# One 256-column value product per key group in a neighbourhood-attention block

## The chip, the core and the metric

The kernel runs on one core of a Trainium2 chip. Its time is the device time of one execution in microseconds (us), median of the runs. The work is spread over TensorE (PE in the profile: matrix products; PEld: loading their stationary operand), VectorE (DVE), ScalarE (ACT), GpSimd (POOL) and SyncE (SP, which here only issues DMAs). Each engine takes its instructions in order and waits on semaphores for the others.

## The reference

One encoder layer over 1024 tokens (a grid of 16 rows and 64 columns) of 1024 channels, in float32:

```python
h = h + 0.5 * swiglu(rms_norm(h, ffn1_norm[i]), ffn1_w_gate[i], ffn1_w_up[i], ffn1_w_down[i])
u = rms_norm(h, mix_norm[i])
q, k, v, s_in, gates = jnp.split(u @ w_in[i], splits, axis=-1)
y_attn = neighbourhood_attention(q, k, v, na_rpb[i]) @ w_attn_out[i]
y_ssm = s5_branch(s_in, ...) @ w_ssm_out[i]
h = h + (sigmoid(gate_a) * y_attn + sigmoid(gate_s) * y_ssm) @ w_out[i]
h = h + 0.5 * swiglu(rms_norm(h, ffn2_norm[i]), ...)
h = h + (p[i] @ ple_w_proj[i]) * jax.nn.sigmoid(rms_norm(h, ple_norm[i]) @ ple_w_gate[i])
return rms_norm(h, final_norm)
```

The attention has 8 heads of 64 channels. Each token sees 8 x 16 neighbours, clamped inside the grid, with a learned bias per head; then softmax over these 128 scores and a weighted sum of the values.

## The kernel before

Activations lie channel-major: 128 channels on the partitions, tokens along the columns. Nearly all products are made in three parts for precision (`mm3`, L182): an operand is split into a rounded part and its remainder (`split`, L152: a cast on ACT, a subtraction on DVE), and hi x hi, hi x lo and lo x hi are summed in PSUM. The order of PE's instructions is the order of the program text (`manual_schedule`, L1796); ACT, DVE and the DMA queues are ordered by a planner that simulates the engines. Only the first stretch and the very end (`end`, L1678) have ACT and DVE in written order as well.

The stages are: feed-forward block 1 (to about 690 us), the mixer (input projections, gates, attention, state-space branch, to about 1170 us), the two branch outputs with gates and the output projection, feed-forward block 2, then the per-layer input and the last norm.

In the mixer the main line of PE is a row of projections (`proj`, L1037: 24 products of 512 columns each) for q, k and the 16 gate tiles. Between these, the generator `mixer_side` (L1286) places the attention and the state-space work: after each so many products `tick` lets it go one step. An attention **unit** is one head, one half of the rows (`rb`) and one of four column blocks (`cb`); there are 64 units, 16 for each pair of heads. In step j the generator puts out:

- the scores of unit j (`attn_scores`, L1198): two products of 288 or 384 columns with the query as the stationary operand; the smallest of the negated scores on DVE (L1211), exponent, sum and scaling on ACT and DVE (L1214 to L1216);
- the turn of unit j-3 (`attn_turn`, L1219): three transposes of 128 columns into one PSUM bank, then a cast on ACT into `pth` (L1226) and the remainder on DVE into `ptl` (L1227);
- the values of unit j-5 (`attn_values`, L1230): for each of three key groups a product of 128 columns with the value's two parts side by side as the stationary operand (128 wide, L1235) and `pth`, and one of 128 columns with the high part alone (64 wide, L1237) and `ptl`. The four column blocks of a head half fill one PSUM bank `O`; after the fourth, ACT copies its lower half out (L1241), DVE adds the upper one in token order (L1242), and ACT issues the store to `o_d` (L1245);
- two steps of the state-space scan on POOL; from unit 49 on also `ssm_out` (L1097), whose products (`yo`) follow the unit's.

`qk_proj` (L1134) makes the operands of two heads: for each head one query tile `qs` of 1024 columns, keys `kh` and `kl`; for each half of the tokens a PSUM bank is copied out by ACT and DVE. Weights, `qs`, `kh`, `kl` and a few others share a ring `w` of 12 tiles of 4 KB per partition; a large ring `x` of 56 tiles of 2 KB holds the normed activations and most short-lived tiles; a ring `tmp` holds four.

`load_br` (L1400) later loads `o_d` for the branch products and splits it. At the end of the program, `rstd` (L204) computes a reciprocal root on ACT and refines it with three DVE steps; `scaled` (L1654) multiplies by a gain on ACT.

Of the kernel before, what the change touches and what calls it, by code (L numbers as in the profile page):

```python
# [8 lines left out]
F32 = mybir.dt.float32  # L9
# [29 lines left out]
def encoder_block(ctx, tc, I, out):  # L39
# [73 lines left out]
    a2_d = dtile("a2_d", [NF // 2, 7, P, HT])  # L113
    h2_d = dtile("h2_d", [P, NK * SEQ])
    v_d = dtile("v_d", [SEQ, 512])
    o_d = dtile("o_d", [512, SEQ])
    g_d = dtile("g_d", [16, P, SEQ])
    y_d = dtile("y_d", [NPD, P, NCH])
    y2_d = dtile("y2_d", [512, SEQ])
# [81 lines left out]

        return tc.issue_after(mark["ins"]) if "ins" in mark else nullcontext()

    def rstd(m, r, q):  # L204
        A.activation(r, m, AF.Abs_reciprocal_sqrt, bias=eps)
        V.tensor_tensor(q, r, r, ALU.mult)
        V.scalar_tensor_tensor(q, m, eps, q, ALU.add, ALU.mult)
        V.scalar_tensor_tensor(r, q, -3.0, r, ALU.add, ALU.mult)

    class Norm:  # L210
# [33 lines left out]
        def stat(self, r=None, summed=False):  # L244
            if summed:
                m = self.acc
            else:
                m = bank("ms")[:, 0:self.n]
                sums = [self.acc] + self.more
                for i, sq in enumerate(sums):  # L250
                    T.matmul(m, lhsT=ones, rhs=sq, start=i == 0, stop=i == len(sums) - 1)
            q = tmq("rq", [P, self.n])
            r = thid("rs", [P, self.n], F32) if r is None else r
            rstd(m, r, q)
            self.r = r

        def apply(self, gi, res, every):
# [774 lines left out]
    win = I["win"]  # L1032
    ap_cm = tc.tile_pool(name="ap", bufs=1, reuse_waits="tile")
    ap_ = ap_cm.__enter__()
    cur.update(st=(ap_, "st", 3), w=(ap_, "w", 12), tmp=(ap_, "tmp", 4))

    def proj(w, t, name):  # L1037
        o = bank(name)
# [95 lines left out]
    def qk_proj(hp, wq, wk):  # L1134
        qs, kh, kl = [], [], []
        for t in range(2):
            o = proj(wq, t, "q")
            for i in range(2):
                if t == 0:
                    qs.append(tw("qs"))  # L1140
                src = o[i * 64:(i + 1) * 64].rearrange("p (r b c) -> p r b c", r=8, b=4)
                hs, ls = slice(i * 64, (i + 1) * 64), slice((1 - i) * 64, (2 - i) * 64)

                def view(sl):
                    return qs[i][sl, hsl(t)].rearrange("p (b r c) -> p r b c", b=4, r=8)
                A.copy(view(hs), src)
                V.tensor_tensor(view(ls), src, view(hs).bitcast(F32), ALU.subtract)
        for t in range(2):
            o = proj(wk, t, "k")
            for i in range(2):  # L1150
                if t == 0:
                    kh.append(tw("kh"))
                    kl.append(tw("kl"))
                hs, ls = slice(i * 64, (i + 1) * 64), slice((1 - i) * 64, (2 - i) * 64)
                A.activation(kh[i][hs, hsl(t)], o[hs], AF.Copy, scale=0.125)
                A.activation(kh[i][ls, hsl(t)], o[hs], AF.Copy, scale=0.125)
                for s_ in (hs, ls):
                    V.scalar_tensor_tensor(kl[i][s_, hsl(t)], o[hs], 0.125, kh[i][hs, hsl(t)].bitcast(F32),
                                           ALU.mult, ALU.subtract)
        for i in range(2):  # L1160
            qkv[2 * hp + i] = (qs[i], kh[i], kl[i])

    def load_v(hd, cb):
        n = 4 * KNC[cb]
# [33 lines left out]
    def attn_scores(hd, rb, cb):  # L1198
        q, kh, kl = qkv[hd]
        n = KNC[cb]  # L1200
        nk = 12 * n
        qv = q[:, rb * HT + cb * P:rb * HT + (cb + 1) * P]

        def kv(kt):
            return kt.rearrange("p (r c) -> p r c", c=GRID)[:, 4 * rb:4 * rb + 12, KC0[cb]:KC0[cb] + n]
# [13 lines left out]
    def attn_turn(cb, sm):  # L1219
        kp = 4 * KNC[cb]  # L1220
        tp = bank("pt")
        for g in range(3):
            T.transpose(tp[0:kp, ksl(g)], sm[:, g * kp:(g + 1) * kp], ident)
# [6 lines left out]
    def attn_values(hd, rb, cb, O, ph, pl):  # L1230
        kp = 4 * KNC[cb]
        hl = vld[hd, cb]
        for g in range(3):

            T.matmul(O[:, ksl(cb)], lhsT=hl[0:kp, rb + g].rearrange("p h d -> p (h d)"), rhs=ph[0:kp, ksl(g)], start=(g == 0), stop=False,  # L1235
                     skip_group_check=True)
            T.matmul(O[0:64, ksl(cb)], lhsT=hl[0:kp, rb + g, 0], rhs=pl[0:kp, ksl(g)], start=False, stop=(g == 2),  # L1237
                     skip_group_check=True)
        if cb == 3:
            ot, ol = tmp("ot"), tmp("ol")  # L1240
            A.copy(ol[0:64], O[64:128])  # L1241
            V.tensor_tensor(ot[0:64].rearrange("p (r b c) -> p b r c", r=8, b=4),  # L1242
                            O[0:64].rearrange("p (b r c) -> p b r c", b=4, r=8),
                            ol[0:64].rearrange("p (b r c) -> p b r c", b=4, r=8), ALU.add)
# [41 lines left out]
    def mixer_side():  # L1286
# [113 lines left out]
    def load_br(t, b):  # L1400

        res = []
        if b == 0:
            for k in range(0, 4, 2):
                st = tst("br")
                nc.sync.dma_start(st.rearrange("p (k c) -> p k c", k=2),
                                  o_d[k * P:(k + 2) * P, hsl(t)].rearrange("(k p) c -> p k c", p=P))
                for i in range(2):
                    hi, lo = tx("bh"), tx("bl")
                    split(hi, lo, st[:, hsl(i)])  # L1410
                    res.append((hi, lo))
            return res
        for k in range(4):
# [264 lines left out]
    def end():  # L1678
# [131 lines left out]
```

## Time and profile before

| | us |
|---|---|
| median of 3 runs | 2099.88 (2099.48 to 2100.86) |
| profiled execution, its own time | 2096.29 |
| its span (first to last instruction) | 2094.5 |
| PE busy | 2074.5 |
| DVE busy | 1416.1 |
| ACT busy | 999.6 |
| POOL busy | 399.4 |

The granted TensorE clock was 0.998. All sums below are made against the profiled execution; its own time is 3.6 us under the median. PE's products are pipelined: the time from one product's start to the next one's start is what it costs, not its own duration. A timeline row reads: start, duration, engine, line, operation, out<-in, rows*columns of the stationary operand, partitions x columns of the moving one, count. A windows row gives, for a stretch, the sum of its length and each engine's busy time and instructions.

### The profile page before, as it was taken

The numbers are of one execution on the slowest core, as the hardware profiler recorded it, in microseconds if no ns is written. First come the engines' busy times: TensorE is split into PE (matmuls) and PEld (weight loads), VectorE is DVE, ScalarE is ACT, GpSimd is POOL, SyncE is SP. The second block draws the span as 40 slices with busy tenths as digits, with TensorE's granted clock in tenths as the row PEclk, the third lists the DMA queues.
The fourth block names the chain that finished last, engine by engine and source line by source line (L and its number), as shares of the span: only waits on it lengthen the run. The fifth ranks groups of instructions, "written<-read, shape, count | busy, mean of one in ns | idle before, by whom it ended". The sixth has DMA issues, their size and how long they took to land.

```text
span 2094.5 us, 28063 instructions
## 1 busy us (share of the span) xinstructions
PE 2074.5 (99%) x9662; PEld 1705.4 (81%) x9662; DVE 1416.1 (68%) x2420; ACT 999.6 (48%) x1832; POOL 399.4 (19%) x636
## 2 busy tenths in 40 slices
PE   8999999999999999999999999999999999999998
PEld 3788888888888888888898888788888888888886
DVE  7897776667967334677753668995665665786855
ACT  6434333334445333667774635643333334445543
POOL 0037556441000006888200001000000000000000
PEclk9999999999999999999999999999999999999999
DMA  3435444475533551233477745243324238433302
GB/s 134 143 118 154 125 135 120 144 270 169 188 114 111 159 189 64 70 97 98 123 208 260 247 145 117 77 150 121 100 86 135 82 121 297 155 106 94 118 21 81
DMA packets 197744, 285.19 MB, mean 136 GB/s; under 512 B 41569, under 2 KB 81121, under 8 KB 197601
## 3 DMA queue, kind: packets, MB, share of 16 engines
q1 hardware_dynamic: 180304, 258.20, 38.8%
q10 hardware_dynamic: 14992, 21.00, 3.0%
q0 software_dynamic: 2304, 4.20, 1.2%
q8 instruction: 76, 1.25, 0.2%
q14 instruction: 68, 0.55, 0.1%
HBM read 201.01 MB, written 82.31 MB: 135 GB/s over the span
## 4 chain that ended last, share of the span: by engine, by line
PE 94%; DVE 2%; ACT 1%; DMA 1%; SPq 0%; issue 0%; DVEq 0%; ACTq 0%
PE dx L184 4%; PE dx L185 4%; PE dx L186 4%; PE gx L184 3%; PE ux L184 3%; PE ux L186 3%; PE gx L186 3%; PE gx L185 3%; PE ux L185 3%; PE gt L184 3%; PE gt L185 3%; PE gt L186 3%; PE dy L186 2%; PE dy L184 2%; PE dy L185 2%; PE gy L184 2%
## 5 line engine op out<-in xcount | busy, mean ns | idle before, releaser
L153 ACT CAST wh<-hbuf 128x512 fp32r<-128x512 f32 x280 | 173.0, 622 | 392.3 <-PE gx L185 80.9
L154 DVE TENSOR_TENSOR wl<-hbuf,wh 128x512 fp32r<-128x512 f32 x280 | 209.2, 750 | 122.7 <-ACT wh L153 120.5
L153 ACT CAST wh<-wblk 128x512 fp32r<-128x512 f32 x190 | 118.0, 622 | 192.6 <-PE dx L185 83.2
L154 DVE TENSOR_TENSOR wl<-wblk,wh 128x512 fp32r<-128x512 f32 x190 | 130.6, 690 | 49.3 <-ACT wh L153 41.8
L184 PE MATMUL dx<-ah,wh 128*128 128x512 f32 x416 | 163.3, 393 | 0.3 <-DVE hbuf L688 0.3
L186 PE MATMUL dx<-ah,wl 128*128 128x512 f32 x416 | 161.9, 389 | 0.0
L185 PE MATMUL dx<-al,wh 128*128 128x512 f32 x416 | 161.8, 389 | 0.0
L1092 POOL TENSOR_TENSOR sc<-X,rho 128x128 f32<-128x128 f32 x128 | 77.9, 609 | 327.2 <-ACT X L1075 317.3
L154 DVE TENSOR_TENSOR al<-araw,ah 128x512 fp32r<-128x512 f32 x154 | 106.3, 694 | 50.1 <-PE dx L185 21.1
L184 PE MATMUL gx<-xh,wh 128*128 128x512 f32 x320 | 124.9, 390 | 1.2 <-DVE c L575 1.2
L184 PE MATMUL ux<-xh,wh 128*128 128x512 f32 x320 | 125.0, 390 | 0.0
L186 PE MATMUL ux<-xh,wl 128*128 128x512 f32 x320 | 124.5, 389 | 0.0
L185 PE MATMUL gx<-xl,wh 128*128 128x512 f32 x320 | 124.5, 389 | 0.0
L186 PE MATMUL gx<-xh,wl 128*128 128x512 f32 x320 | 124.5, 389 | 0.0
L185 PE MATMUL ux<-xl,wh 128*128 128x512 f32 x320 | 124.5, 389 | 0.0
L153 ACT CAST ah<-araw 128x512 fp32r<-128x512 f32 x154 | 94.9, 619 | 43.2 <-PE dx L185 12.6
L184 PE MATMUL gt<-xh,wh 128*128 128x512 f32 x256 | 102.7, 401 | 0.0
L186 PE MATMUL gt<-xh,wl 128*128 128x512 f32 x256 | 99.8, 390 | 0.0
L185 PE MATMUL gt<-xl,wh 128*128 128x512 f32 x256 | 99.8, 390 | 0.0
L422 DVE TENSOR_TENSOR hbuf<-hbuf 128x512 f32<-128x512 f32 x120 | 91.4, 762 | 2.1
L184 PEld LDWEIGHTS dx<-ah,wh 128*128 128x128 f32 x416 | 78.1, 188 | 17.8 <-issue 0.7
L185 PEld LDWEIGHTS dx<-al,wh 128*128 128x128 f32 x416 | 78.1, 188 | 16.9 <-issue 0.7
(381 smaller groups left out, 5590.2 us busy)
## 6 DMA issues: line engine op xcount, KB each, us to landing
araw<-a_d SPq DMA_DIRECT2D x154, 256.0 KB
a_d<-c SPq DMA_DIRECT2D x148, 256.0 KB
wblk<-in_wd SPq DMA_DIRECT2D x88, 256.0 KB
hbuf<-in_wg SPq DMA_DIRECT2D x40, 512.0 KB
hbuf<-in_wu SPq DMA_DIRECT2D x40, 512.0 KB
wst<-in_win SPq DMA_DIRECT2D x26, 512.0 KB
hbuf<-in_xT SPq DMA_DIRECT2D x32, 256.0 KB
h_d<-hbuf ACTq DMA_DIRECT2D x32, 256.0 KB
```

What stands on the lines that cost most here:

```text
L153: A.copy(hi, src)
L154: return eng.tensor_tensor(lo, src, hi.bitcast(F32), ALU.subtract)
L184: T.matmul(o, lhsT=wh, rhs=xh, start=first, stop=False, skip_group_check=more)
L185: T.matmul(o, lhsT=wh, rhs=xl, start=False, stop=False, skip_group_check=more)
L186: T.matmul(o, lhsT=wl, rhs=xh, start=False, stop=last, skip_group_check=more)
L422: V.tensor_tensor(b11, (b12, b22, None, None, b21)[i - 2], b11, ALU.subtract)
L1092: G.tensor_tensor(sc, both, rho4, ALU.mult)
```

## The change

- The turn writes one tile `ptb` of 3 x 2 x 128 columns, high and low part of each key group side by side, in a ring of its own of two tiles. `attn_values` then makes one product of 256 columns for each key group, with the 128-wide stationary operand (the low x low quarter is computed too, and not used). A bank `O` holds two column blocks now instead of four, each with its two parts.
- After each second block ACT copies both halves of the high part into a tile `ot` (one buffer) in token order, and DVE adds the low part to the upper half. `o_d` has two planes: all 128 rows of `ot` are stored, and `load_br` loads both planes and adds them on DVE.
- In `mixer_side` the values of unit j-5 come ahead of the turn of unit j-3.
- Queries are kept by token half, in tiles of the ring `x`; the ring `w` has 10 tiles.
- At the end, two gain multiplications on ACT come behind the reciprocal root (`mid`) instead of ahead of it.

```diff
-    o_d = dtile("o_d", [512, SEQ])
+    o_d = dtile("o_d", [2, 512, SEQ])
...
-    def rstd(m, r, q):
+    def rstd(m, r, q, mid=None):
         A.activation(r, m, AF.Abs_reciprocal_sqrt, bias=eps)
+        if mid is not None:
+            mid()
         V.tensor_tensor(q, r, r, ALU.mult)
...
-    cur.update(st=(ap_, "st", 3), w=(ap_, "w", 12), tmp=(ap_, "tmp", 4))
+    cur.update(st=(ap_, "st", 3), w=(ap_, "w", 10), tmp=(ap_, "tmp", 4))
...
             for i in range(2):
-                if t == 0:
-                    qs.append(tw("qs"))
+                q = thid("qs")
+                qs.append(q)
...
-        qv = q[:, rb * HT + cb * P:rb * HT + (cb + 1) * P]
+        qv = q[rb][:, ksl(cb)]
...
-        ph = thid("pth", [P, 384])
-        pl = thid("ptl", [P, 384])
-        A.copy(ph[0:kp], tp[0:kp, 0:384])
-        V.tensor_tensor(pl[0:kp], tp[0:kp, 0:384], ph[0:kp].bitcast(F32), ALU.subtract)
-        return ph, pl
+        pb = ap_.tile([P, 3, 2, P], F32R, tag="ptb", bufs=2, name="ptb")
+        src = tp[0:kp, 0:384].rearrange("p (g q) -> p g q", g=3)
+        A.copy(pb[0:kp, :, 0], src)
+        V.tensor_tensor(pb[0:kp, :, 1], src, pb[0:kp, :, 0].bitcast(F32), ALU.subtract)
+        return pb
...
+        o = O["o"][:, (cb % 2) * 256:(cb % 2) * 256 + 256]
         for g in range(3):
-            T.matmul(O[:, ksl(cb)], lhsT=hl[0:kp, rb + g].rearrange("p h d -> p (h d)"), rhs=ph[0:kp, ksl(g)], start=(g == 0), stop=False,
+            T.matmul(o, lhsT=hl[0:kp, rb + g].rearrange("p h d -> p (h d)"), rhs=pb[0:kp, g].rearrange("p h q -> p (h q)"), start=(g == 0), stop=(g == 2),
                      skip_group_check=True)
-            T.matmul(O[0:64, ksl(cb)], lhsT=hl[0:kp, rb + g, 0], rhs=pl[0:kp, ksl(g)], start=False, stop=(g == 2),
-                     skip_group_check=True)
+        if cb % 2 == 0:
+            return
+        if cb == 1:
+            O["t"] = ap_.tile([P, HT], F32, tag="ot", bufs=1, name="ot")
+        ov = O["t"].rearrange("p (r b c) -> p b r c", r=8, b=4)[:, cb - 1:cb + 1]
+        src = O["o"].rearrange("p (b h r c) -> p h b r c", b=2, h=2, r=8)
+        A.copy(ov[64:128], src[64:128, 0])
+        A.copy(ov[0:64], src[0:64, 0])
+        V.tensor_tensor(ov[0:64], src[0:64, 1], ov[0:64], ALU.add)
         if cb == 3:
-            ot, ol = tmp("ot"), tmp("ol")
-            A.copy(ol[0:64], O[64:128])
-            V.tensor_tensor(ot[0:64].rearrange("p (r b c) -> p b r c", r=8, b=4),
-                            O[0:64].rearrange("p (b r c) -> p b r c", b=4, r=8),
-                            ol[0:64].rearrange("p (b r c) -> p b r c", b=4, r=8), ALU.add)
-            nc.scalar.dma_start(o_d[hd * 64:(hd + 1) * 64, hsl(rb)], ot[0:64])
+            nc.scalar.dma_start(o_d[:, hd * 64:(hd + 1) * 64, hsl(rb)], O["t"])
...
+            if 0 <= j - 5 < n:
+                hd, rb, cb = units[j - 5]
+                if cb % 2 == 0:
+                    O.setdefault((hd, rb), {})["o"] = bank("O")
+                attn_values(hd, rb, cb, O[hd, rb], pts.pop(j - 5))
+                if rb == 1 and hd + 1 < NH:
+                    load_v(hd + 1, cb)
             if 0 <= j - 3 < n:
                 pts[j - 3] = attn_turn(units[j - 3][2], sms.pop(j - 3))
-            if 0 <= j - 5 < n:
-                hd, rb, cb = units[j - 5]
-                if cb == 0:
-                    O[hd, rb] = bank("O")
-                attn_values(hd, rb, cb, O[hd, rb], *pts.pop(j - 5))
-                if rb == 1 and hd + 1 < NH:
-                    load_v(hd + 1, cb)
...
-                st = tst("br")
-                nc.sync.dma_start(st.rearrange("p (k c) -> p k c", k=2),
-                                  o_d[k * P:(k + 2) * P, hsl(t)].rearrange("(k p) c -> p k c", p=P))
+                st = [tst("br") for _ in range(2)]
+                for w in range(2):
+                    nc.sync.dma_start(st[w].rearrange("p (k c) -> p k c", k=2),
+                                      o_d[w, k * P:(k + 2) * P, hsl(t)].rearrange("(k p) c -> p k c", p=P))
+                V.tensor_tensor(st[0], st[0], st[1], ALU.add)
...
         A.activation(dummy, eps, AF.Abs_reciprocal_sqrt)
-        scaled(6, six[3])
         added(a, b, s, hm)
         fin[2].square(7, V)
-        scaled(7, hm)
         finish(1, (4, 6))
-        fin[2].stat()
+        fin[2].stat(mid=lambda: (scaled(6, six[3]), scaled(7, hm)))
```

On PE, a unit beside a gate tile stood so before (s: scores, pt: transposes, O: values, gt: the gate tile's products):

```order
L186 MATMUL gt<-xh,wl 128x512
L1207 MATMUL s<-kh,qs 128x384
L1208 MATMUL s<-kl,qs 128x384
L1223 MATMUL pt<-ident,sm 96x128 x3
L1235 MATMUL O<-pth,vhl 128x128
L1237 MATMUL O<-ptl,vhl 64x128
L1235 MATMUL O<-pth,vhl 128x128
L1237 MATMUL O<-ptl,vhl 64x128
L1235 MATMUL O<-pth,vhl 128x128
L1237 MATMUL O<-ptl,vhl 64x128
L184 MATMUL gt<-xh,wh 128x512
```

and stands so now:

```order
L186 MATMUL gt<-xh,wl 128x512
L1209 MATMUL s<-kh,qs 128x384
L1210 MATMUL s<-kl,qs 128x384
L1239 MATMUL O<-ptb,vhl 128x256 x3
L1225 MATMUL pt<-ident,sm 96x128 x3
L184 MATMUL gt<-xh,wh 128x512
```

Six products of 128 columns became three of 256, ahead of the transposes; the rest of PE's row is the same in both kernels.

The second place is DVE at the seam between two pairs of heads, from the end of the work behind the scores of unit 15 to those of unit 17, the first that needs the new keys (sm: the row that first reads the scores, kl: the new keys' remainder, of which PE's scores of unit 17 read kl_8033 before and kl_8011 now, wl: a weight's remainder). Before:

```order
L1158 SCALAR_TENSOR_TENSOR kl_8039<-k_7918,kh_8038 64x512 x2
L1215 RECIPROCAL stat_8100<-stat_8100 128x1
L1158 SCALAR_TENSOR_TENSOR kl_8033<-k_8044,kh_8032 64x512 x2
L154 TENSOR_TENSOR wl_8139<-wst_8136,wh_8138 128x1024
L1211 ISA sm_8155,stat_8156<-s_8152,tb_7985 128x288
L1211 ISA stat_8156 128x1
L154 TENSOR_TENSOR wl_8553<-wst_8550,wh_8552 128x1024
L1227 TENSOR_TENSOR ptl_8166<-pt_8161,pth_8165 96x384
```

Now:

```order
L1217 RECIPROCAL stat_8074<-stat_8074 128x1
L1229 TENSOR_TENSOR ptb_8090<-pt_8086,ptb_8090 96x3x128
L154 TENSOR_TENSOR wl_8113<-wst_8110,wh_8112 128x1024
L1213 ISA sm_8129,stat_8130<-s_8126,tb_7968 128x288
L1213 ISA stat_8130 128x1
L1160 SCALAR_TENSOR_TENSOR kl_8011<-k_8022,kh_8010 64x512 x2
L1195 TENSOR_TENSOR tb_8172<-row_8164,colm_6143 128x12x24
L154 TENSOR_TENSOR wl_8503<-wst_8500,wh_8502 128x1024
```

The pair that unit 17 still needs (kl_8033 before, kl_8011 now; the second token half of the pair's first head) stands behind unit 16's score row sm_8129 now, where it stood ahead of it. The pair of the other head's first token half (kl_8039 in the first row before) now stands ahead of unit 15's score row, outside this piece. At unit 33 the rows are the same; at unit 49 two copies of the scan's state stand ahead of the key pair as well.

More of the change, by code (lines that the diff above doesn't have):

```diff
@@ L242, in bring, with stat @@
             self.rest = sq
-        def stat(self, r=None, summed=False):
+        def stat(self, r=None, summed=False, mid=None):
             if summed:
@@ L253, in stat @@
             r = thid("rs", [P, self.n], F32) if r is None else r
-            rstd(m, r, q)
+            rstd(m, r, q, mid)
             self.r = r
@@ L1144, in view @@
                 def view(sl):
-                    return qs[i][sl, hsl(t)].rearrange("p (b r c) -> p r b c", b=4, r=8)
+                    return q[sl].rearrange("p (b r c) -> p r b c", b=4, r=8)
                 A.copy(view(hs), src)
@@ L1160, in qk_proj @@
         for i in range(2):
-            qkv[2 * hp + i] = (qs[i], kh[i], kl[i])
+            qkv[2 * hp + i] = (qs[i::2], kh[i], kl[i])
     def load_v(hd, cb):
@@ L1223, in attn_turn, with attn_values @@
             T.transpose(tp[0:kp, ksl(g)], sm[:, g * kp:(g + 1) * kp], ident)
[L1224 to L1230 removed]
+        pb = ap_.tile([P, 3, 2, P], F32R, tag="ptb", bufs=2, name="ptb")
[3 more added lines that the diff above has]
+        return pb
+    def attn_values(hd, rb, cb, O, pb):
         kp = 4 * KNC[cb]
         hl = vld[hd, cb]
+        o = O["o"][:, (cb % 2) * 256:(cb % 2) * 256 + 256]
         for g in range(3):
[L1235 removed]
+            T.matmul(o, lhsT=hl[0:kp, rb + g].rearrange("p h d -> p (h d)"), rhs=pb[0:kp, g].rearrange("p h q -> p (h q)"), start=(g == 0), stop=(g == 2),
                      skip_group_check=True)
[L1237 to L1245 removed]
+        if cb % 2 == 0:
[7 more added lines that the diff above has]
+        V.tensor_tensor(ov[0:64], src[0:64, 1], ov[0:64], ALU.add)
+        if cb == 3:
+            nc.scalar.dma_start(o_d[:, hd * 64:(hd + 1) * 64, hsl(rb)], O["t"])
     ydr = y_d.rearrange("g (t o) c -> g o t c", o=16)
@@ L1404, in load_br @@
             for k in range(0, 4, 2):
-                st = tst("br")
-                nc.sync.dma_start(st.rearrange("p (k c) -> p k c", k=2),
-                                  o_d[k * P:(k + 2) * P, hsl(t)].rearrange("(k p) c -> p k c", p=P))
+                st = [tst("br") for _ in range(2)]
[3 more added lines that the diff above has]
+                V.tensor_tensor(st[0], st[0], st[1], ALU.add)
                 for i in range(2):
                     hi, lo = tx("bh"), tx("bl")
-                    split(hi, lo, st[:, hsl(i)])
+                    split(hi, lo, st[0][:, hsl(i)])
                     res.append((hi, lo))
```

## The prediction

> **What bounds the kernel now.** I read the page first: its head, the busy times, and the chain of work that ended last (section 4).
>
> ```profile
> span 2094.5 us, 28063 instructions
> PE 2074.5 (99%) x9662; PEld 1705.4 (81%) x9662; DVE 1416.1 (68%) x2420; ACT 999.6 (48%) x1832; POOL 399.4 (19%) x636
> ...
> PE 94%; DVE 2%; ACT 1%; DMA 1%; SPq 0%; issue 0%; DVEq 0%; ACTq 0%
> ```
>
> PE is busy in 99% of the span and is 94% of the chain. An average can hide a stage with another limit, so I looked at the attention's stretch in windows of 20 us (columns: length, then busy time and count of PE, PEld, DVE, ACT, POOL, then clock, DMA share, GB/s).
>
> ```profile
> 880.00:900.00 20.00, 20.00 (x119) 17.39 (x118) 17.62 (x38) 16.38 (x35) 17.26 (x36) 1.00 0.31 91
> 900.00:920.00 20.00, 20.00 (x119) 17.34 (x118) 12.82 (x34) 13.21 (x31) 17.18 (x37) 1.00 0.34 93
> ...
> 1020.00:1040.00 20.00, 19.34 (x131) 17.30 (x131) 12.72 (x36) 12.96 (x31) 0.00 (x0) 1.00 0.58 170
> ...
> 1080.00:1100.00 20.00, 19.60 (x142) 17.74 (x141) 7.32 (x18) 12.86 (x28) 0.00 (x0) 1.00 0.78 233
> ...
> 1120.00:1140.00 20.00, 20.00 (x90) 16.57 (x89) 5.84 (x9) 7.63 (x12) 0.00 (x0) 1.00 0.87 329
> ```
>
> In a quiet stretch (900 to 920) PE is full, DVE stands at 12.8 and ACT at 13.2 of 20. At a seam between two pairs of heads (880 to 900), with new queries and keys to split, DVE is at 17.6 and ACT at 16.4: little room there. PE idles 0.66 us in one window and 0.40 in another, both beside the state-space products. So what PE gives up in this stretch is time won, as long as the other engines keep up.
>
> **The term that counts: the values on PE.** "Busy" says nothing of a small product's cost, since products overlap. I take start to start. This is PE's timeline of one unit behind its scores, and of PEld's stationary loads in it:
>
> ```profile
> 902.01 0.49 PE L1223 MATMUL pt<-ident,sm 128*96 128x128 f32 x3
> 902.25 0.31 PE L1235 MATMUL O<-pth,vhl 128*128 128x128 f32 x1
> 902.39 0.22 PE L1237 MATMUL O<-ptl,vhl 128*64 128x128 f32 x1
> 902.46 0.27 PE L1235 MATMUL O<-pth,vhl 128*128 128x128 f32 x1
> 902.57 0.22 PE L1237 MATMUL O<-ptl,vhl 128*64 128x128 f32 x1
> 902.63 0.27 PE L1235 MATMUL O<-pth,vhl 128*128 128x128 f32 x1
> 902.74 0.23 PE L1237 MATMUL O<-ptl,vhl 128*64 128x128 f32 x1
> 902.80 0.45 PE L184 MATMUL gt<-xh,wh 128*128 128x512 f32 x1
> 903.08 0.40 PE L185 MATMUL gt<-xl,wh 128*128 128x512 f32 x1
> ```
>
> ```profile
> 902.40 0.19 PEld L1235 LDWEIGHTS O<-pth,vhl 128*128 128x128 f32 x1
> 902.51 0.14 PEld L1237 LDWEIGHTS O<-ptl,vhl 128*64 128x64 f32 x1
> 902.57 0.19 PEld L1235 LDWEIGHTS O<-pth,vhl 128*128 128x128 f32 x1
> ```
>
> From the first transpose to the second gate product are 1.07 us. The loads start 0.11 apart behind a 128-wide one and 0.06 behind a 64-wide one, and the products step in the same rhythm (0.11, 0.06): the values are paced by loading their stationary operands, 0.17 per key group.
>
> What the new row costs I put together from two pieces that the trace has. Transposes with a gate tile right behind them, no values, stand at the first units:
>
> ```profile
> 844.65 0.49 PE L1223 MATMUL pt<-ident,sm 128*96 128x128 f32 x3
> 844.89 0.48 PE L184 MATMUL gt<-xh,wh 128*128 128x512 f32 x1
> 845.21 0.39 PE L185 MATMUL gt<-xl,wh 128*128 128x512 f32 x1
> ```
>
> That is 0.56 us from the first transpose to the second gate product. And products of 256 columns with a new 128-wide stationary operand each stand at the end of the program:
>
> ```profile
> 2067.85 0.28 PE L184 MATMUL pg<-xh,whh 128*128 128x256 f32 x1
> 2067.85 0.19 PEld L185 LDWEIGHTS pg<-xl,whh 128*128 128x128 f32 x1
> 2067.97 0.28 PE L185 MATMUL pg<-xl,whh 128*128 128x256 f32 x1
> ```
>
> They start 0.12 apart, each with its own load beside the product before it. Since 0.12 is over the 0.11 of a load, the load is hidden. A unit goes from 1.07 to 3 x 0.12 + 0.56 = 0.92: 0.15 won; with the rounding of the rows 0.15 to 0.16, and I take 0.155. Over 64 units: 64 x 0.155 = **9.9 us**.
>
> The Trainium skill's page "TensorE: Matmul & The Clock Gate" gives, under "Back-to-back issue gap", columns / 2.4 + 2.5 ns, so 109 ns for 256 columns. By that the unit would win 0.18 and the sum would be 11.8 us; the rows above say 0.12, and I stay with them.
>
> **The other terms.** *Copies out of PSUM.* The rows by form, in the attention's stretch (the 128x256 and 128x1024 adds: the program's last stretch):
>
> ```profile
> L1241 ACT COPY ol<-O 64x512 f32<-64x512 f32 x16 | 9.3, 584 | 1.8 <-PE yo L1119 1.5
> ...
> L1121 ACT COPY ys<-yo 128x256 f32<-128x256 f32 x16 | 5.9, 366 | 3.2 <-PE yo L1119 1.8 <-DMA y_d<-ys 1.2
> ```
>
> ```profile
> L1242 DVE TENSOR_TENSOR ot<-O,ol 64x512 f32<-64x512 f32 x16 | 10.9, 680 | 4.3 <-ACT ol L1241 4.2
> ```
>
> ```profile
> L1671 DVE TENSOR_TENSOR hbuf<-hbuf,rs 128x1024 f32<-128x1024 f32 x4 | 4.6, 1220 | 0.0
> ...
> L1651 DVE TENSOR_TENSOR ps<-ps,pp 128x256 f32<-128x256 f32 x4 | 1.7, 414 | 0.0
> ```
>
> ACT had 16 copies of 0.584 (9.3 us) and gets 64 of 256 columns at about 0.366 (23.4): 14 us more over some 265 us, or 1.1 in a window of 20. DVE had 16 adds of 0.680 (10.9) and gets 32 at 0.414 (13.2): 2.4 more. Neither reaches 20 even at a seam (ACT 17.5, DVE 17.8). On the path: nothing, because scores are made three units ahead of their turn, about 11 us; without that cover the 14 us of ACT would be PE's.
>
> *Keys at the seams.* Here the order on DVE moved: the keys that unit 17 needs are behind unit 16's score row now. Times of DVE and PE at this seam:
>
> ```profile
> 890.04 0.29 PE L1207 MATMUL s<-kh,qs 128*128 128x288 f32 x1
> ...
> 893.88 0.29 PE L1207 MATMUL s<-kh,qs 128*128 128x288 f32 x1
> ```
>
> ```profile
> 892.54 0.45 DVE L1211 CUSTOM_DVE_ANT_1 sm<-s,tb 128x288 f32<-128x288 f32 x1
> ...
> 895.18 1.40 DVE L1158 SCALAR_TENSOR_TENSOR kl<-k,kh 64x512 fp32r<-64x512 f32 x2
> ```
>
> DVE came to unit 16's scores 2.50 us after PE had begun them. If it is as late again, the keys behind them (0.45 + 1.40) are ready 4.35 after; PE wants them at 3.84 - 0.155 = 3.69. That is 0.66 lost, three times: 2.0 us. But of the four key remainders (two pairs, 2.8 us) that stood ahead of that row and made it late, none stands between units 15 and 16 now; with DVE only half of that (1.4) earlier there are 0.7 to spare. Between 0 and 2.0 I take 0.3, near the end that the order speaks for.
>
> *Values ahead of the turn.* A part of the weights is used two units after it is made, as before, less the 0.36 that the values now come earlier; that costs nothing against two units of 3.8. The new ring of two tiles costs nothing either: the turn's cast waits for its transposes, and the values that free its tile stand ahead of these on PE.
>
> *One tile `ot`.* Its next first copy must wait for the store of the last contents. A store of 128 KB from ACT's queue is on the chain of waits with
>
> ```profile
> 1031.79 2.98 DMA y_d<-ys
> ```
>
> so 256 KB take 3.0 to 6.0 us (as an estimate: the same, or twice that). With two copies and an add ahead of it (2 x 0.37 + 0.41 = 1.15) that is 4.1 to 7.1, against two units of 3.84 = 7.7. It fits where DVE is not late. I take 0.
>
> *The second plane of `o_d`.* Four DVE adds of 1.22, and 2 MB more each way. In the window 1120 to 1140 PE is full with gates and DVE has 14 us free, so 0.
>
> *The end.* The root on ACT stood behind two gain multiplications:
>
> ```profile
> 2084.47 1.28 DVE L1671 TENSOR_TENSOR hbuf<-hbuf,rs 128x512 f32<-128x512 f32 x2
> 2084.57 0.89 ACT L1655 ACTIVATE hbuf<-hbuf,gains 128x256 f32<-128x256 f32 x2
> 2084.60 0.70 PE L251 MATMUL ms<-sq,ones 128*128 128x256 f32 x2 [0.70 <-DVE sq L232]
> ...
> 2085.85 0.42 DVE L206 TENSOR_TENSOR rq<-rs 128x256 f32<-128x256 f32 x1
> ```
>
> The sum on PE that the root reads ends at 2085.30 anyway, and DVE, which goes on with the root, is itself busy until 2085.75 and went on at 2085.85. At most 0.1 is won; I take 0.05.
>
> Sum: -9.9 + 0.3 - 0.05 = -9.65. From the profiled execution's 2096.29 that is 2086.6; its own time lies 3.6 under the runs' median, so against the median of 2099.88 I forecast **2090.2 us**.
>
> **Rivals.** *A second wait at the seams and beside the state-space products.* The keys cost their 2.0, and the waits of 1020 to 1100 (0.66 + 0.40) double, since ACT's copies come on top there: 3.1 together in place of 0.3, so 2093.0. For it: 17.6 of 20 on DVE at a seam. Against it: the stretch gives back tiles, since the parts of the attention weights leave the large ring and the copies of `O` leave `tmp`.
>
> *The single `ot` paces the attention.* ACT takes its work in order; if the copy stands for a store, the exponents behind it stand too. With DVE 2.5 late the 4.1 to 7.1 become 6.6 to 9.6, up to 1.9 over the two units at each of 15 reuses. The three units of advance take most of that; half a microsecond left on PE each time gives 7.5 back: 2097.7, no difference. It decides once ACT is late by more than the advance of about 11 us.
>
> *The new products do not hide their loads*: slower. If a load may start only when the product before it is through, a value product costs 0.12 + 0.11 = 0.23 and a unit 0.69 + 0.56 = 1.25 in place of 1.07: 64 x 0.18 = 11.5 lost, 2111.4. The point: steps of over 0.17 between value products. Against it stand the rows at 2067.85, where a load starts with the product before it and the next product starts 0.12 on. The Trainium skill's page "TensorE: Matmul & The Clock Gate", Part 3, "The mechanism", says that loads overlap with products in flight only where their row groups differ; by that rule this case would come; the trace disagrees, since those operands fill all 128 rows.
>
> **How the numbers follow.** The forecast has a chance of 0.68 (its own range 2088.5 to 2091.5: 0.15 to 0.165 a unit, 0 to 1 of waits), the second wait 0.16, the single `ot` 0.10, exposed loads 0.06. A measurement of this kernel tells 0.2% (4.2 us) from no change: faster means under 2095.7. The first two cases are faster, 0.84; the third is the same, 0.10; the last slower, 0.06. For 8 in 10 the range runs from 2087.5 (0.16 a unit, the 1.06 of idle gone, and 1.0 for the spread of the runs) to 2095.0, past the second case toward the third.
>
> **What would show it.** Right: value products 0.12 apart and scores 0.15 to 0.16 closer from unit to unit; PE without waits in the units; span 9 to 10 us shorter, and all of that between 845 and 1110; the end as before. Wrong: PE waiting for kl or kh at units 17, 33 and 49; ACT's copies into `ot` waiting for the store of `o_d`; idle PE beside the state-space products above 1.1; branch products later than the 9.9 earlier that they should be.

## The result, and the profile after

The changed kernel takes 2151.3 us (median of 6 runs, 2148.66 to 2154.26); the kernel before, beside it, 2099.8. The ratio is 1.0245, with a 95% interval of 1.0232 to 1.0258: 51.5 us slower, where 9.65 faster were forecast. The profiled execution took 2149.13 us.

The head, the busy times and the chain of waits of the changed kernel:

```profile
span 2147.4 us, 27774 instructions
...
PE 2087.0 (97%) x9470; PEld 1708.6 (80%) x9470; DVE 1420.4 (66%) x2440; ACT 1006.8 (47%) x1880; POOL 401.7 (19%) x636
...
PE 77%; DMA 10%; DVE 7%; ACT 3%; issue 2%; SPq 0%; ACTq 0%; DVEq 0%
PE dx L184 4%; PE dx L185 4%; PE dx L186 4%; DMA o_d<-ot 4%; PE ux L184 3%; PE ux L185 3%; PE ux L186 3%; PE gx L184 3%; PE gx L185 3%; PE gx L186 3%; PE dy L186 2%; PE dy L185 2%; PE dy L184 2%; PE uy L184 2%; PE gy L184 2%
```

PE fell from 94% of the chain to 77%, DMA rose from 1% to 10%, and one transfer, the store of `ot`, is 4% of the span by itself. On PE the new row does what was forecast of it. A unit in the changed kernel (PE's timeline):

```profile
906.65 0.34 PE L1209 MATMUL s<-kh,qs 128*128 128x384 f32 x1
906.82 0.34 PE L1210 MATMUL s<-kl,qs 128*128 128x384 f32 x1
907.00 0.53 PE L1239 MATMUL O<-ptb,vhl 128*128 128x256 f32 x3
907.37 0.49 PE L1225 MATMUL pt<-ident,sm 128*96 128x128 f32 x3
907.61 0.47 PE L184 MATMUL gt<-xh,wh 128*128 128x512 f32 x1
907.93 0.39 PE L185 MATMUL gt<-xl,wh 128*128 128x512 f32 x1
```

Three value products take 0.37, so 0.12 each, and from the first of them to the second gate product are 0.93, where 0.92 was forecast and 1.07 stood before. What went wrong is in the waits. The first rows are those of all engines, the others PE's own (line waited for: us in total, times, longest):

```profile
DVE ot L1250 <- ACT ot L1249: 47.9, 19, 7.2
ACT ot L1248 <- DMA o_d<-ot: 42.9, 12, 5.6
...
DVE br L1416 <- DMA br<-o_d: 13.0, 3, 5.7
```

```profile
PE O L1239 <- DVE ptb L1229: 11.7, 6, 4.9
PE yo L1119 <- DMA emi<-u_d: 9.8, 4, 3.0
PE s L1210 <- DVE kl L1160: 5.8, 3, 2.9
PE s L1209 <- ACT kh L1158: 5.3, 3, 2.1
```

ACT stood 12 times, 42.9 us in all, for the store of the last contents of the single tile `ot`. The chain between 864 and 892 us shows two turns of that:

```profile
864.31 0.37 ACT ot L1248
...
865.54 10.65 DMA o_d<-ot
876.27 0.37 ACT ot L1248
876.65 0.37 ACT ot L1249
...
882.49 0.37 ACT ot L1248
...
883.96 7.92 DMA o_d<-ot
891.96 0.37 ACT ot L1248
```

Store, first copy, the second copy two units later, store: the next store goes out 18.4 us after the last, where four units take about 15.0 when nothing waits (3.70 to 3.81 each). The windows show what it costs PE (columns as in the prediction):

```profile
860.00:900.00 40.00, 36.48 (x190) 31.31 (x189) 29.20 (x68) 27.42 (x65) 34.36 (x73) 0.97 0.23 71
900.00:940.00 40.00, 37.12 (x191) 31.54 (x191) 23.34 (x64) 23.24 (x59) 34.52 (x71) 0.99 0.33 97
940.00:980.00 40.00, 35.67 (x179) 29.98 (x178) 26.44 (x61) 25.84 (x61) 34.04 (x77) 0.96 0.25 81
980.00:1020.00 40.00, 36.90 (x187) 31.47 (x186) 24.26 (x65) 24.10 (x61) 28.61 (x56) 0.96 0.35 99
1020.00:1060.00 40.00, 34.92 (x184) 29.87 (x184) 24.25 (x64) 28.67 (x69) 0.00 (x0) 0.91 0.29 81
1060.00:1100.00 40.00, 31.85 (x193) 28.10 (x192) 19.21 (x56) 22.14 (x59) 0.00 (x0) 0.96 0.57 167
1100.00:1140.00 40.00, 34.27 (x209) 30.23 (x208) 17.68 (x49) 22.76 (x58) 0.00 (x0) 0.96 0.60 173
1140.00:1170.00 30.00, 25.13 (x105) 20.38 (x104) 7.00 (x12) 14.97 (x25) 0.00 (x0) 0.89 0.61 166
...
1200.00:1240.00 40.00, 35.81 (x150) 28.93 (x149) 22.88 (x29) 21.17 (x31) 0.00 (x0) 0.96 0.76 226
```

The idle times of PE in these nine windows add up to 41.9 us. The granted clock is down in all of them, and from its shares (40 x 0.03, 40 x 0.01 and so on) up to another 16.5 us are lost (a little less, since PE also idles in a part of that time). That is up to 58.4 us in all, and nearly the whole loss: the kernel below with the first copies of X on POOL, which has the same products without these waits, spans 60.3 us less.

**Why the store is slow.** The transfers' own records in the trace tell it (worked out from the first ten stores of each kernel; the completion packets are those of 4 bytes that end a transfer):

| kernel | data packets of 2 KB | completion packets | last data packet after the issue, median (range) |
|---|---|---|---|
| before, one plane of 64 rows | 64 | 16 | 2.2 us (1.9 to 2.6) |
| after, two planes of 64 rows | 128 | 2 | 8.6 us (7.6 to 10.3) |
| two planes, one transfer each | 2 x 64 | 2 x 16 | 3.2 us (2.7 to 5.2), from the first issue |
| 128 rows in one run | 128 | 16 | 2.3 us (1.6 to 3.1) |

The records do not number the transfer engines, but they show how many packets were under way at a time: on the average 7 to 12 in a store of the kernel before, 1.6 to 2.1 in one over two planes, which also ends with 2 completion packets and not 16. So this store went through 2 of 16 engines, with 64 packets behind one another on each. The Trainium skill's page "DMA: Bandwidth & Descriptors", section "Why a DMA increments its semaphore by 16 and not by 1", states the rule: a transfer issued this way uses the largest number of engines up to 16 that divides the slowest dimension of both sides. For a target whose slowest dimension is the two planes that is 2, and the trace agrees, with its 2 completion packets. The prediction did not weigh that rule.

### The profile page after: what moved, and what is told of

Read it like the earlier page. It is cut to its first block, busy times and chain, and to the rows that moved or that the text cites. A ratio compares the mean times of both kernels' runs of the same rounds, so it can differ in the third digit from the quotient of the medians.

```text
span 2147.4 us, 27774 instructions
## 1 busy us (share of the span) xinstructions
PE 2087.0 (97%) x9470; PEld 1708.6 (80%) x9470; DVE 1420.4 (66%) x2440; ACT 1006.8 (47%) x1880; POOL 401.7 (19%) x636
## 4 chain that ended last, share of the span: by engine, by line
PE 77%; DMA 10%; DVE 7%; ACT 3%; issue 2%; SPq 0%; ACTq 0%; DVEq 0%
PE dx L184 4%; PE dx L185 4%; PE dx L186 4%; DMA o_d<-ot 4%; PE ux L184 3%; PE ux L185 3%; PE ux L186 3%; PE gx L184 3%; PE gx L185 3%; PE gx L186 3%; PE dy L186 2%; PE dy L185 2%; PE dy L184 2%; PE uy L184 2%; PE gy L184 2%
## 5 line engine op out<-in xcount | busy, mean ns | idle before, releaser
L153 ACT CAST ah<-araw 128x512 fp32r<-128x512 f32 x154 | 94.9, 619 | 45.2 <-PE dx L185 12.6
L184 PE MATMUL gt<-xh,wh 128*128 128x512 f32 x256 | 107.4, 420 | 2.2 <-DVE ptb L1229 1.4
```

The source lines that it names most:

```text
L153: A.copy(hi, src)
L184: T.matmul(o, lhsT=wh, rhs=xh, start=first, stop=False, skip_group_check=more)
```

## The experiments

Three questions were put. Is the loss the store, or the rings and seams? Does a single `ot` stall with a quick store too? And why do the gains of a quick store at first not show? The ratio is to the kernel before, beside the same runs (2098.9 to 2099.3 us).

| run | us | ratio (95%) |
|---|---|---|
| store as two transfers | 2096.66 | 0.9989 (0.9979 to 0.9999) |
| `ot` in the ring of five | 2135.97 | 1.0181 (1.0164 to 1.0198) |
| before, with the moved buffers alone | 2097.80 | 0.9997 (0.9988 to 1.0007) |
| sum before the store | 2100.73 | 1.0014 (1.0004 to 1.0023) |
| 128 rows in one run | 2099.22 | 1.0003 (0.9993 to 1.0012) |
| two transfers, outputs from step 50 | 2093.36 | 0.9970 (0.9960 to 0.9981) |
| sum before the store, step 50 | 2098.85 | 0.9999 (0.9990 to 1.0009) |
| before, step 50 | 2096.17 | 0.9988 (0.9979 to 0.9997) |
| two transfers, first copies of X on POOL | 2089.39 | 0.9953 (0.9938 to 0.9968) |
| two transfers, all copies of X on POOL | 2091.65 | 0.9960 (0.9947 to 0.9973) |
| before, first copies on POOL | 2097.09 | 0.9992 (0.9982 to 1.0001) |
| sum before the store, first copies on POOL | 2090.56 | 0.9965 (0.9952 to 0.9978) |

### The store

Two transfers instead of one, `ot` still a single tile:

```diff
-            nc.scalar.dma_start(o_d[:, hd * 64:(hd + 1) * 64, hsl(rb)], O["t"])
+            for w in range(2):
+                nc.scalar.dma_start(o_d[w, hd * 64:(hd + 1) * 64, hsl(rb)], O["t"][w * 64:(w + 1) * 64])
```

> The changed kernel with one edit: the store of ot is issued as two transfers, one for each plane of o_d, 64 rows each, the shape that the kernel before stored with; ot stays one tile. Theory (a store over two planes lands late, 7.9 to 10.7 us in the chain of waits, and ACT, in order, waits for it with all that is behind it): the landing falls to about 3 us plus the second issue, the two waits of ACT and DVE on ot (42.9 and 47.9 us of idle time) all but vanish, 2090 to 2094. Rival (one tile for all units paces the attention however short the store is): 2110 or more. Rival (the loss is in the rings, the queries or the seams, not in the store): within 10 us of 2151.

55 us came back: 2096.66 us, 2.7 above the range of the theory. ACT waits no more for the store, so a single `ot` is enough for a store of 3.2 us: 3.2 + 7.5 (two units) + 1.9 (copies and add) is 12.6, under four units. What kept the other microseconds is told under "POOL's recursion".

The other way to mend it, with the layout: one transfer of the same 128 rows and bytes, the rows of a head in one run.

```diff
-    o_d = dtile("o_d", [2, 512, SEQ])
+    o_d = dtile("o_d", [8, P, SEQ])
...
-            nc.scalar.dma_start(o_d[:, hd * 64:(hd + 1) * 64, hsl(rb)], O["t"])
+            nc.scalar.dma_start(o_d[hd, :, hsl(rb)], O["t"])
...
-                    nc.sync.dma_start(st[w].rearrange("p (k c) -> p k c", k=2),
-                                      o_d[w, k * P:(k + 2) * P, hsl(t)].rearrange("(k p) c -> p k c", p=P))
+                    for h in range(2):
+                        nc.sync.dma_start(st[w][h * 64:(h + 1) * 64].rearrange("p (k c) -> p k c", k=2),
+                                          o_d[2 * k + h:2 * k + h + 3:2, w * 64:(w + 1) * 64, hsl(t)].rearrange("k p c -> p k c"))
```

> The changed kernel with one edit: o_d is laid out with the 128 rows of a head one after the other, so that the one store of ot, with the same 128 rows of 2 KB, is one run of rows and not two planes; the branch is read with two transfers for each one of before. Theory (the store was late since its packets went through 2 of 16 transfer engines, and that comes from the two planes as the outermost dimension, not from the bytes or the rows): the landing falls under 4 us, the waits on ot vanish, within 3 us of the run with two stores, 2093 to 2100. Rival (twice the bytes in one transfer are slow however they lie): landing 7 us or more and 2140 or more.

It landed after 2.3 us, through all 16 engines, and the kernel took 2099.22 us. So neither the bytes nor the number of rows made the store slow; the two planes in front did. This version lies 2.6 us behind the two transfers, and its waits say where: PE stands once, 3.0 us, for the branch's operands, which 16 loads bring now.

```profile
PE s L1210 <- DVE kl L1160: 3.0, 1, 3.0
PE br L184 <- ACT bh L153: 3.0, 1, 3.0
```

Then the single tile was taken away and the slow store left:

```diff
-    cur.update(st=(ap_, "st", 3), w=(ap_, "w", 10), tmp=(ap_, "tmp", 4))
+    cur.update(st=(ap_, "st", 3), w=(ap_, "w", 10), tmp=(ap_, "tmp", 5))
...
-            O["t"] = ap_.tile([P, HT], F32, tag="ot", bufs=1, name="ot")
+            O["t"] = tmp("ot")
```

> The changed kernel with one edit: ot is taken from the ring of 512-column tiles that rows, value columns and stored steps also use, five tiles instead of four, and not from a tile of its own; the one store over both planes stays. Theory (late store times a single tile): a store that lands after 8 to 11 us no longer holds the next unit but one that comes a turn of the ring later, 2092 to 2105, with the store in the queue still as long as before. Rival (slow stores hurt by holding the queue or the transfers' engines, whatever buffer they come from): 2125 or more. Rival (rings and seams): within 10 us of 2151.

A miss: 2135.97, not 2092 to 2105, and in the range of the rival in which slow stores hurt whatever buffer they come from. The slow store holds a place of the ring now, and whoever comes to that place next waits for it, DVE's bias rows most of all:

```profile
DVE row L1188 <- DMA o_d<-ot: 15.8, 4, 7.6
```

A store of 9 us is expensive in a ring of five too, if less than in a ring of one. How much of the 37 us that are left comes from the ring's places and how much from the transfers themselves was not separated. The cure is the transfer, not one tile more.

The rival that the moved buffers cost by themselves:

```diff
-    cur.update(st=(ap_, "st", 3), w=(ap_, "w", 12), tmp=(ap_, "tmp", 4))
+    cur.update(st=(ap_, "st", 3), w=(ap_, "w", 10), tmp=(ap_, "tmp", 4))
...
-                if t == 0:
-                    qs.append(tw("qs"))
+                q = thid("qs")
+                qs.append(q)
...
```

> The kernel before with only the move of the buffers: queries by token half in the large ring and ten weight tiles instead of twelve; values, output tiles and store as before. Theory: between 0 and 2 us above the kernel before, 2100 to 2103. Rival (this part costs the attention or the weights their advance): 2110 or more. Rival (the ten weight tiles bring nothing up to a loss only with the shorter units): 2100.

2097.80, ratio 0.9997: nothing that can be told from no change. The rival that the moved buffers cost something is out.

Last, a version that keeps the store of one plane and sums the parts first:

```diff
...
+        ol = ap_.tile([64, 256], F32, tag="ot", bufs=1, name="ol")
+        olv = ol.rearrange("p (b r c) -> p b r c", b=2, r=8)
...
-        A.copy(ov[64:128], src[64:128, 0])
-        A.copy(ov[0:64], src[0:64, 0])
+        A.copy(olv, src[64:128, 0])
+        V.tensor_tensor(ov[0:64], src[0:64, 0], olv, ALU.add)
         V.tensor_tensor(ov[0:64], src[0:64, 1], ov[0:64], ALU.add)
...
-            nc.scalar.dma_start(o_d[:, hd * 64:(hd + 1) * 64, hsl(rb)], O["t"])
+            nc.scalar.dma_start(o_d[hd * 64:(hd + 1) * 64, hsl(rb)], O["t"][0:64])
...
```

> The changed kernel, but the three parts of the product are summed before the store: ACT copies the upper half of the 256-column product (64 rows by 256) to a small tile, DVE adds it and the third part, the store has one plane of 64 rows as in the kernel before, and the branch is loaded as before. Theory: the gain on PE (64 units by 0.155 us) is kept and neither the store nor the transition grows, 2088 to 2093; DVE has one addition more of 64 by 256 at each second step. Rival (DVE's lag at the scores grows by that addition): 2095 to 2105. Rival (rings and seams): 2140 or more.

2100.73: no store is late here, and yet no gain. The time lies in the range of the rival that DVE's added work costs it; a run under the next heading decides that. With the store mended, two quite different kernels had lost about 7 and 10 us somewhere else, which made one common place likely.

### POOL's recursion

The place is one seam. Windows of the kernel with two transfers:

```profile
1000.00:1020.00 20.00, 15.54 (x85) 13.25 (x84) 13.79 (x33) 14.27 (x34) 14.77 (x34) 1.00 0.23 67
1020.00:1040.00 20.00, 20.00 (x115) 17.68 (x114) 12.40 (x35) 13.51 (x35) 0.00 (x0) 0.91 0.53 143
1040.00:1060.00 20.00, 19.00 (x129) 17.25 (x128) 12.80 (x40) 17.71 (x46) 0.00 (x0) 1.00 0.77 227
```

PE idles 4.5 us in one window, has a clock of 0.91 in the next (1.8 us of 20) and idles 1.0 more: 7.3 of the forecast 9.65. The Trainium skill's page "TensorE: Matmul & The Clock Gate", Part 1, "What's actually happening", says that the clock halves after an idle window of about 3.4 us; the trace agrees: 0.91 over 20 us is half the clock for 3.6 us, right behind a gap of 4.5. The chain of waits in this stretch is POOL's, and it leads over the copies of the state X into the keys and PE's scores:

```profile
1014.08 0.37 POOL X L1096
1014.52 0.52 POOL sc L1094
1016.20 0.51 DVE xs L1113
1016.74 0.46 DVE sm L1213
1017.84 0.68 DVE kl L1160
1018.53 0.70 DVE kl L1160
1019.27 0.40 PE s L1210
```

POOL runs the 128 steps of the state-space recursion by itself from about 800 to 1010 us; nothing speeds it up when PE gets faster. The first copies of X stand on DVE ahead of the keys of unit 49 (the part on the change names those two copies). The recursion's last operation and the copies (duration min/median/max, then first and last start), before and with two transfers:

```profile
L1094 POOL TENSOR_TENSOR X<-sc,X x128: 342/363/1230, 799.3 to 1009.9; 128x64 f32<-128x64 f32 x128
...
L1111 ACT COPY xs<-X x32: 388/403/409, 1015.3 to 1080.3; 64x256 f32<-64x256 f32 x32
L1111 DVE COPY xs<-X x32: 286/289/292, 1017.3 to 1079.4; 64x256 f32<-64x256 f32 x32
```

```profile
L1096 POOL TENSOR_TENSOR X<-sc,X x128: 326/366/2029, 801.3 to 1017.0; 128x64 f32<-128x64 f32 x128
...
L1113 DVE COPY xs<-X x32: 286/289/507, 1015.9 to 1083.5; 64x256 f32<-64x256 f32 x32
L1113 ACT COPY xs<-X x32: 395/404/410, 1015.9 to 1084.3; 64x256 f32<-64x256 f32 x32
```

Before, POOL was through some 5 us ahead of the first copy. With shorter units DVE came to it about 5 us earlier (it began to wait at 1012.4), and POOL ended 7 us later, 5 of them because the recursion itself took longer (215.7 us and not 210.6). Both were needed: with its length of before it would have ended at about 1012, and next to nothing would have waited for it. Three runs tried a later step for the outputs:

```diff
-        SO = 48
+        SO = 50
```

> The changed kernel with the store as two transfers (as in the run of two stores), and the outputs of the state space taken up from attention step 50 instead of 48. Theory (the faster units reach the copies of X at step 48 before POOL has ended the recursion: DVE sat 3.5 us and ACT 3.0 us for X, the keys' second parts stood behind on DVE, PE lost 4.5 us and then clock): the wait of DVE and ACT on X vanishes or falls under 1 us, PE's wait for kl goes, 2088.5 to 2092. Rival (the seam with its keys stalls by itself, whatever POOL does): the wait for kl stays at 3 to 5 us, 2095 to 2098. Rival (the outputs pressed into fewer steps cost at the end what the start gains): no wait for X, but 2094 to 2098.

> The kernel that sums the three parts before the store (one plane), with the outputs of the state space from step 50 instead of 48. Theory (there DVE and ACT sat 6.0 and 5.9 us for X, and PE 7.0 us for kl): POOL ends at 1019 us there, so most of the 7.0 us and the clock lost behind go, 2090 to 2094. Rival (the extra addition on DVE is what costs): 2097 or more.

> The kernel before with the outputs of the state space from step 50 instead of 48, nothing else. Theory (in the kernel before no copy of X waited for POOL, so the step has nothing to give): within 2 us of the kernel before, 2097 to 2101. Rival (a later step is better in itself, and the gain of the run with both edits is not of the shorter units): 2094 or less. Rival (outputs pressed into the end of attention cost): 2102 or more.

The edit missed its aim. In both kernels with the wide products DVE still waited for X (3.5 us in the first), and PE for `kl`:

```profile
PE s L1210 <- DVE kl L1160: 3.8, 1, 3.8
```

The planner had put the first two copies in the same place of DVE's order, behind a weight's remainder and ahead of a score row; only the second pair moved. The kernel before gained 2.8 us from the step, a little more than expected (its 1.1 us of idle PE beside the state-space products went); the two others 3.3 and 1.9. So this step is a small gain for any of them and no test of POOL.

The better test takes the first copies off the waiting engines. POOL makes them, behind its own recursion:

```diff
-                (A.copy if g == r else V.tensor_copy)(xs[r * 64:(r + 1) * 64, g], both)
+                (G.tensor_copy if pr < 2 else A.copy if g == r else V.tensor_copy)(xs[r * 64:(r + 1) * 64, g], both)
```

> The changed kernel with the store as two transfers, and the copies of the state X for the first two outputs of the state space on POOL, behind the recursion that makes X, instead of on ACT and DVE; step 48 as in the changed kernel. Theory (with the shorter units DVE and ACT come to these copies 3 to 4 us before POOL has ended, the keys of unit 49 stand behind them on DVE, and PE loses 4.5 us and 2 to 3 us by a lower clock behind it): no engine but POOL waits for X, PE's wait for kl at unit 49 goes, 2088.5 to 2092. Rival (the seam stalls by itself): PE waits 3 us or more for kl there, 2095 to 2098. Rival (the shorter units make another wait at once): 2093 to 2096.

> The kernel before with the copies of X for the first two outputs on POOL, nothing else. Theory (its longer units come to these copies after POOL has ended, so nothing was lost there; only the 1.1 us of idle PE beside the state-space products can move): within 1.5 us of the kernel before with a later step, 2095 to 2099. Rival (the copies on ACT and DVE cost the kernel before as much as the changed one): 2094 or less.

With two transfers: **2089.39 us, 0.9953 (0.9938 to 0.9968)**, faster than both kernels of this case and inside the range of the theory. Its windows:

```profile
980.00:1020.00 40.00, 40.00 (x216) 34.71 (x215) 32.34 (x78) 31.37 (x75) 34.54 (x74) 1.00 0.35 98
1020.00:1060.00 40.00, 38.45 (x249) 34.71 (x248) 24.57 (x73) 31.26 (x81) 0.27 (x1) 1.00 0.71 206
```

The seam is full, the clock whole; 1.55 us stay beside the state-space products, where PE waits for a load (`emi`). The kernel before gets nothing from the same edit that could be told from no change (0.9992). So these copies, on ACT and DVE, cost the kernel with the shorter units 7.3 us and the kernel before 2.2, which cannot be told from nothing, as the theory has it. The same edit for the sum ahead of the store, and all copies on POOL:

> The kernel that sums the three parts before the store (one plane), with the copies of X for the first two outputs on POOL. Theory: its 7.0 us of wait for kl and the clock lost behind them go, 2090 to 2094. Rival (the addition on DVE keeps PE waiting elsewhere): 2096 or more.

> As the run before, with all 64 copies of X on POOL. Theory: the same, 2088 to 2092, if four copies on POOL take less than a unit of 3.8 us each time; ACT and DVE have 11 us and 9 us less to do between 1015 and 1085. Rival (a POOL copy of 64 by 256 takes over 0.95 us): PE waits for xs at the state-space products, 2094 or more.

The first went from 2100.73 to 2090.56: the missing 10 us came back, and the extra addition on DVE was not its trouble. In the second a copy on POOL took 0.40 us, and 2091.65 cannot be told from the run with two pairs on POOL.

## Why the prediction was wrong

*The step that failed* is "One tile `ot`", taken as 0. Its criterion was right: landing plus copies against two units of 7.7 us. Its landing, 3.0 to 6.0 us, was scaled by bytes from another store. Measured were 7.6 to 10.3, so with 1.15 of copies and add 8.8 to 11.5 and not 4.1 to 7.1: 1.1 to 3.8 us over the two units at each reuse, where nothing was expected. Doubling the bytes was harmless (2.3 us in one run of 128 rows); the leading dimension of two was not, and no row of the trace before showed such a store.

*The rival "the single `ot` paces the attention"* named the mechanism and put it at 7.5 us; it was up to 58. Two of its steps fell. "With DVE 2.5 late" was the wrong source: the store itself was late. And "the three units of advance take most of that" fails in kind: store, copy, two units, copy, store is a loop, so what it is too long comes again each time, and advance is spent once. From the first store to the sixteenth, one took 19.3 us (865.5 to 1155.1) where the kernel before took 16.2:

```profile
L1252 ACTq DMA_DIRECT2D o_d<-ot x16: 491/497/1078, 865.5 to 1155.1; - x16
```

```profile
L1245 ACTq DMA_DIRECT2D o_d<-ot x16: 452/453/507, 865.9 to 1108.3; - x16
```

The loss is a little more than 15 x (19.3 - 16.2), about 47 us, since the kernel should have been faster than before here.

*Values on PE*, -9.9: right in mechanism, a little large. The pieces are 0.12 and 0.93 as forecast. From scores to scores, though, a unit won 0.13 to 0.14, not 0.155: the rest is given back by the 512-column products behind that piece (last section), whose steps the sum took as unchanged. In the kernel with the first copies on POOL two such steps stand at

```profile
905.37 0.29 PE L1209 MATMUL s<-kh,qs 128*128 128x288 f32 x1
...
909.07 0.29 PE L1209 MATMUL s<-kh,qs 128*128 128x288 f32 x1
```

3.70 against 3.84 before. The median step over all units is 3.80 against 3.93; at 0.13 the 64 units give 8.3.

*Exposed loads* (2111.4, the slower rival): wrong, value products step 0.12 apart. *A second wait at the seams and beside the state-space products* (2093.0): once the store is quick, such waits are what is left, and in these places, but they took 7.3 us and not 3.1, and neither the order of the keys nor ACT's copies out of PSUM made them. *Keys at the seams*, 0.3 with bounds of 0 and 2.0: with the store mended, units 17 and 33 stall nowhere, so the order there cost nothing; unit 49 lost 4.5 us of waiting, 7.3 with the clock and the waits behind, by DVE's wait for POOL's X. That lies outside the bounds. The part on the change saw the two copies of the state ahead of this key pair, and the prediction asked what DVE had to do there, not whether X would be ready. POOL, at 19% of the span, stood in the prediction's own windows with 17.2 of 20 and was passed over.

*Copies out of PSUM, values ahead of the turn, second plane*: the first two cost nothing that shows once the store is quick; PE is full from 820 to 1020 in the best version. The second plane is not free in each form: with 16 loads it cost PE 3.0. *The end* (0.05) is too small to be told.

*The sum.* Two small sums in the prediction do not come out of their own terms: 64 x 0.18 is 11.5, not 11.8, and 0.165 a unit with no waits gives 2089.3 as the lower end of the forecast's own range, not 2088.5. The forecast does not hang on either. With the store as two transfers and the first copies on POOL the kernel takes 2089.39, where 2090.2 was forecast for it. Part of that is chance: against the kernel before with the same copies it is 7.7 faster, about the 8.3 of PE's steps (the waits beside the state-space products are alike in both, 1.5 and 1.6), and not 9.65; the other 2.2 are what that edit moved in the kernel before, which cannot be told from nothing.

## What to carry to other kernels

When a tile of one buffer is stored and filled again, add up the loop (fill, store, landing, next fill) and set it against the time in which the work comes round; if it is longer, advance elsewhere does not help, and the landing must be looked up for that very layout: count the engines that a transfer uses, not its bytes. Let the leading dimension of a store be the rows (or issue one transfer for each plane). And before the bound engine is made faster, list the engines that keep a pace of their own beside it, here POOL's recursion, and ask which queue reaches their results first.

## What was not expected of the hardware

- 256 KB through 2 engines took 8.6 us, through 16 engines 2.3 us, with the same 128 packets of 2 KB; as two transfers of one plane 3.2 us. The Trainium skill's page "DMA: Bandwidth & Descriptors", "Rules for kernel authors", says of two transfers for two halves of the partitions not to bother and to use one transfer of 128 partitions. The trace agrees where the one transfer uses 16 engines (2.3 us against 3.2 for two), and differs where it uses 2 (8.6).
- POOL's recursion does not keep its length: 210.6 us from first to last step before and 215.7 with two transfers (rows above), with its last operation taking up to 2.0 us, where its longest was 1.2 before, beside a median of 0.37. It was 210.2 and 215.5 in the two kernels with the first copies on POOL. The records of its 384 operations show where the time goes. Count for each what it takes beyond the quick ones of its line (the 10th percentile): that makes 29.1 us before and 33.4 with two transfers. Of these, 25.1 (89 operations) and 30.7 (82) fall on operations that run at the same time as one of three rows of DVE with two SBUF tiles to read (`wl<-wst,wh`, `tb<-row,colm`, `row<-bt,rowm`), and the added 5 us lie there. No run took these rows away, so this is a coincidence in time and not a cause shown.
- Of the eleven steps between the 512-column products behind the first one of a unit, the first six are 0.228 to 0.236 us long in the kernels with the wide value products (medians over the units between 865 and 1000 us), and the other five 0.227; in the kernel before all eleven are 0.227, at a granted clock of 1.00 in both. Together that is 0.03 a unit, which brings the 0.155 down to the 0.13 measured. Why, no run shows.
